# Putting both maps' score products side by side in a differential attention: a decoder trunk on one Trainium2 core

## The chip, the core and the metric

The kernel runs on one core of one Trainium2 chip. A core has a tensor engine (PE in the profile, with its weight loads as PEld), a vector engine (DVE), a scalar engine (ACT), a GpSimd engine (POOL), and a queue of transfers issued by SyncE (SP). Each engine works through its own instructions in order and waits on semaphores for the others. [...] The metric is the device time of the whole program in microseconds (us), the median of several executions.

## The reference

Two decoder layers over 512 tokens of width 1024, float32, batch 1. Layer 0 is a gated recurrence, layer 1 a differential attention; each is followed by a mixture of 32 experts of which every token uses two. What matters here is the attention (8 heads, each with two maps of 64 dimensions, rows in blocks of 128):

```python
def diff_attention(h, w_in, w_out, lam_params, subln_w, lambda_init):
    ...
    for blk in range(S // Q):
        q0, kend = blk * Q, (blk + 1) * Q
        s = jnp.einsum('bhmqd,bhmkd->bhmqk', q[:, :, :, q0:kend], k[:, :, :, :kend]).astype(jnp.float32) * scale
        mask = (q0 + jnp.arange(Q))[:, None] >= jnp.arange(kend)[None, :]
        p = jax.nn.softmax(jnp.where(mask, s, -jnp.inf), axis=-1)
        a = p[:, :, 0] - lam * p[:, :, 1]
        outs.append(jnp.einsum('bhqk,bhkv->bhqv', a, v[:, :, :kend]))
    ...
    return o.transpose(0, 2, 1, 3).reshape(B, S, D).astype(h.dtype) @ w_out
```

## The kernel before

The order of all instructions is written out by hand with Python generators: `weave(main, (other, rate))` advances `other` by `rate` steps for each step of `main`, and each step appends instructions to the engines' queues. Nothing is reordered later.

The attention (`attention`, lines 583 to 733) works on two halves of four heads. A projection block (`proj`, line 215, and `proj_rows`, line 241) makes Q, K or V of one half from weights that ACT (line 179) and POOL or DVE (line 180) split into a high and a low part. `heads(half, ...)` works through 16 units of a half. A unit is one head `h` and one block `t` of 128 query rows (t = 0 to 3), and so has n = 128(t+1) key columns. Each half has four units of each size, 32 units in all. At step u of `heads` the queues receive:

- `score(u)`: for each of the two maps m, the product of 64 dimensions (partitions 64m to 64m+63 of `qT` and `kT`, line 633), followed by the causal mask, a bf16 product of the identity with a triangle of -1e30 that is added to the last 128 columns (line 634). Each map has a PSUM tile, a bank, of its own. A float32 product shows as two weight loads and two MATMUL records.
- `mix(u-2)`: DVE combines both maps' probabilities (lines 653 to 655), PE transposes the result (line 659), ACT copies it out (line 661).
- `probs(u)`: DVE takes the maximum of each map (line 644), scales it (line 645), ACT makes the exponentials with their sums (line 647). The second exponential is the last to read a unit's score tiles.
- `av(u-3)`: PE multiplies by V (line 668), ACT copies and squares (lines 671, 673).

In half 0 the units go head by head, t = 0 to 3 each, and all use the two tiles `sc0` and `sc1`, so that a unit's first product waits until the unit before has read its first map, and the second product until it has read the second. They are woven with the Q and K projections of half 1 (line 724). In half 1 the units go by t, all four heads of a size together; the first 8 or so are woven with the V projection (line 730), the rest run without a projection beside them (line 731). From its ninth unit on, half 1 uses six tiles in turn (`sc0`, `sc1`, `pj0` to `pj3`). After the last unit come the rest of the output weights, the norm and `mix_out`, then the experts of layer 1.

In the experts (lines 1204, 1205, 1222, 1223), blocks of at most 64 tokens use 64 columns of the array at a time: the products of line 1222 write the first 64 partitions of one bank, those of line 1223 the last 64 of another, one after the other in the queue:

```python
for k in range(NF):
    b, e = (k == 0), (k == NF - 1)
    nc.tensor.matmul(y[0][0:n, :], gt[:, k, 0:n], w[NC1 + k][:, 0:512], start=b, stop=e)
    nc.tensor.matmul(y[1][P - n:P, :], gt[:, k, 0:n], w[NC1 + k][:, 512:1024], start=b, stop=e)
```

Of the kernel before, what the change touches and what calls it, by code (L numbers as in the profile page):

```python
# [9 lines left out]
F32 = mybir.dt.float32  # L10
# [11 lines left out]
S = 512  # L22
P = 128
# [89 lines left out]
def weave(main, *others):  # L113

    due = [0.0] * len(others)
    for n, _ in enumerate(main):
        for i, (g, rate, *start) in enumerate(others):
            due[i] += rate if n >= sum(start) else 0.0
            while due[i] >= 1.0:
                due[i] -= 1.0  # L120
                if next(g, "end") == "end":
                    due[i] = -1e9
# [25 lines left out]
def chain(*gens):  # L148
    for g in gens:
        yield from g  # L150
# [432 lines left out]
def attention(K, pool, psum, st, hh, hl, o):  # L583

    nc = K.nc
    nlam, wn, cos, sin, ident_b, causal = K.attn
    ss, rs = ([K.wp.tile([P, NT, 4], F32, name=f"{n}{i}") for i in range(2)] for n in ("ss", "rs"))
    v = [pool.tile([P, NT, 512], F32, name=f"v{i}") for i in range(2)]
    T, due = {}, []

    def qk_done(name, half):
        def f(t, ps):
            if t == 0:
                T[name, half] = pool.tile([P, 4, S], F32, name=name, bufs=2)
            dst = T[name, half]
            pv = ps.rearrange("p (m w d) -> p m w d", m=8, w=2)
            tt = K.stage.tile([P, 1024], F32, name="raw", bufs=12)
            ta, tb = (tt[:, 512 * j:512 * j + 512].rearrange("p (m w d) -> p m w d", m=8, w=2) for j in range(2))
            for x, f in ((ta, cos), (tb, sin)):
                nc.vector.tensor_tensor(x, pv, f[:, t, None, None, :].to_broadcast([P, 8, 2, 32]), OP.mult)  # L600
            for w in range(2):
                nc.gpsimd.tensor_tensor(ta[:, :, w, :], ta[:, :, w, :], tb[:, :, 1 - w, :],
                                        OP.add if w else OP.subtract)
            tf = tt[:, 0:512]

            def turn():
                tr = psum.tile([P, 4, P], F32, name="tr")
                for h in range(4):
                    nc.tensor.transpose(tr[:, h, :], tf[:, h * P:(h + 1) * P], K.ident)
                nc.scalar.activation(dst[:, :, t * P:(t + 1) * P], tr, AF.Copy)  # L610

            K.later.append(turn)
        return f

    def v_done(half):
        def f(t, ps):
            nc.scalar.activation(v[half][:, t, :], ps, AF.Copy)
        return f

    def heads(half, units, tags, after):  # L620

        qT, kT = T["qT", half], T["kT", half]
        U = {}

        def score(u):
            h, t = units[u]
            names = tags(u)
            n = (t + 1) * P
            sc = []
            for m in range(2):  # L630
                r = slice(64 * m, 64 * m + 64)
                x = psum.tile([P, S], F32, name=names[(2 * u + m) % len(names)])
                nc.tensor.matmul(x[:, 0:n], qT[r, h, t * P:n], kT[r, h, 0:n], start=True, stop=False)
                nc.tensor.matmul(x[:, t * P:n], ident_b, causal, start=False, stop=True)
                sc.append(x)
            U[u] = (h, t, n, sc)

        def probs(u):
            h, t, n, sc = U[u]
            z = pool.tile([P, 10], F32, name="st", bufs=4)  # L640
            mx, nm, l, c, cc = (z[:, 2 * j:2 * j + 2] for j in range(5))
            p = K.stage.tile([P, 1024], F32, name="raw", bufs=12).rearrange("p (m n) -> p m n", m=2)
            for m in range(2):
                nc.vector.tensor_reduce(mx[:, m:m + 1], sc[m][:, 0:n], AX.X, OP.max)
            nc.vector.tensor_scalar(nm, mx, -0.125, None, op0=OP.mult)
            for m in range(2):
                nc.scalar.activation(p[:, m, 0:n], sc[m][:, 0:n], AF.Exp, bias=nm[:, m:m + 1], scale=0.125,
                                     accum_out=l[:, m:m + 1])
            U[u] = (h, t, n, p, l, c, cc)

        def mix(u):
            h, t, n, p, l, c, cc = U[u]
            nc.vector.reciprocal(c, l)
            nc.vector.scalar_tensor_tensor(cc[:, 0:1], c[:, 1:2], nlam, l[:, 0:1], op0=OP.mult, op1=OP.mult)
            nc.vector.scalar_tensor_tensor(p[:, 0, 0:n], p[:, 1, 0:n], cc[:, 0:1], p[:, 0, 0:n],
                                           op0=OP.mult, op1=OP.add)
            tr = psum.tile([P, 4, P], F32, name="tr")
            for s in range(t + 1):
                nc.tensor.transpose(tr[:, s, :], p[:, 0, s * P:(s + 1) * P], K.ident)
            aT = pool.tile([P, 4, P], F32, name="aT", bufs=2)  # L660
            nc.scalar.activation(aT[:, 0:t + 1, :], tr[:, 0:t + 1, :], AF.Copy)
            U[u] = (h, t, c, aT)

        def av(u):
            h, t, c, aT = U.pop(u)
            po = psum.tile([P, S], F32, name="po")
            for s in range(t + 1):
                nc.tensor.matmul(po[:, 0:P], aT[:, s, :], v[half][:, s, h * P:(h + 1) * P],
                                 start=(s == 0), stop=(s == t))
            c0 = (4 * half + h) * P  # L670
            nc.scalar.activation(o[:, t, c0:c0 + P], po[:, 0:P], AF.Copy, scale=c[:, 0:1])
            sq = pool.tile([P, P], F32, name="sq")
            nc.scalar.activation(sq, po[:, 0:P], AF.Square, scale=c[:, 0:1], accum_out=ss[half][:, t, h:h + 1])
            if u in after:
                due.append(after[u])

        for u in range(len(units) + 3):
            if u < len(units):
                score(u)
            if 0 <= u - 2 < len(units):  # L680
                mix(u - 2)
            if u < len(units):
                probs(u)
            if 0 <= u - 3:
                av(u - 3)
            yield

    def finish(half, t0, n, table=False):
        sv, rv = (x[half][:, t0:t0 + n, :].rearrange("p t h -> p (t h)") for x in (ss, rs))
        nc.vector.tensor_scalar(sv, sv, 1.0 / P, EPS, op0=OP.mult, op1=OP.add)  # L690
        yield from rsqrt_steps(K, K.wp, rv, sv, 4 * n, table)
        yield
        for t in range(t0, t0 + n):
            for h in range(4):
                c = slice((4 * half + h) * P, (4 * half + h + 1) * P)
                nc.vector.scalar_tensor_tensor(o[:, t, c], o[:, t, c], rs[half][:, t, h:h + 1], wn,
                                               op0=OP.mult, op1=OP.mult)
            yield

    def finishing(n):  # L700
        for _ in range(n):
            while not due:
                yield
            yield from due.pop(0)

    def turning(steps):

        for _ in steps:
            for turn in K.later[0:2]:
                turn()  # L710
            del K.later[0:2]
            yield

    def block(done):
        return proj(K, st, psum, hh, hl, True, done)

    K.scratch = Ctx()
    K.scratch.lng, K.scratch.lnb = (v[1].rearrange("p t n -> p (t n)")[:, j * D:(j + 1) * D] for j in range(2))
    yield proj_rows(K, st, psum, hh, hl, qk_done("qT", 0))
    weave(chain(block(qk_done("kT", 0)), block(v_done(0))), (K.rows, 0.25))  # L720
    drain(K.rows)
    s0 = heads(0, [(h, t) for h in range(4) for t in range(NT)], lambda u: ["sc0", "sc1"], {15: finish(0, 0, 4)})
    K.lo_eng = nc.gpsimd
    weave(chain(block(qk_done("qT", 1)), block(qk_done("kT", 1))), (s0, 0.7))
    drain(s0)
    s1 = heads(1, [(h, t) for t in range(NT) for h in range(4)],
               lambda u: ["sc0", "sc1"] + ([f"pj{i}" for i in range(4)] if u >= 8 else []),
               {4 * t + 3: finish(1, t, 1) for t in range(NT - 1)})
    f, w = finishing(NT), wout(K, 1)
    weave(turning(proj_rows(K, st, psum, hh, hl, v_done(1))), (s1, 0.9), (f, 1.0))  # L730
    weave(s1, (w, 0.8), (f, 1.0))
    drain(f)
    K.wsteps = chain(iter([None]), w, finish(1, NT - 1, 1, True))
# [977 lines left out]
```

## Time and profile before

| | |
|---|---|
| time, median of 3 runs | 1717.24 us (1713.92 to 1721.87) |
| the profiled execution | 1717.6 us, its span 1715.8 us |
| PE busy | 1464.7 us, 85% of the span |
| DVE, ACT, POOL busy | 657.4, 362.9, 317.4 us (38%, 21%, 18%) |
| mean granted clock of the tensor engine | 0.92 of full speed |
| first score product to the last unit's product with V | 1071.8 to about 1255 us |

The times of stages are counted from the start of the span. [...] A timeline line has start and duration in us, the engine, the line of the code, the operation, what it writes and reads, its shape and how many equal records are merged in it; in brackets is how long the engine sat idle before it and what ended that. Ends of MATMUL records are modelled, so the text counts from start to start.

### The profile page before, as it was taken

The page shows a single profiled execution, that of the slowest core. Times are in us where ns is not written, and L with a number is a line of the kernel's source. Part 1 is how long each engine was busy: PE and PEld are TensorE (multiplying, and loading weights), DVE is VectorE, ACT ScalarE, POOL GpSimd, SP SyncE. Part 2 cuts the span into 40 slices and gives each one's busy share as a digit, 9 for nine tenths or more (in the row PEclk, how much of TensorE's full clock was granted, in tenths as well). Part 3 has the DMA queues.
Part 4 walks back from the last instruction along what each step waited for, and adds up shares of the span by engine and source line. Part 5 has one row for each costly group of instructions (what it writes and reads, how often), then busy time and mean ns, then how long its engine had stood idle before and what let it go on. Part 6 is the DMA issues. An engine that isn't in the chain of part 4 may idle for free. (4 is left out here: it accounts for less than half of the span.)

```text
span 1715.8 us, 22446 instructions
## 1 busy us (share of the span) xinstructions
PE 1464.7 (85%) x6488; PEld 869.9 (51%) x6488; DVE 657.4 (38%) x1486; ACT 362.9 (21%) x754; POOL 317.4 (18%) x299
## 2 busy tenths in 40 slices
PE   6999999988776989988888389999989569989870
PEld 3767776757643434333333268566467334444340
DVE  5335556648750111111112162545577521111105
ACT  2331232123210001101111143453532101000100
POOL 2000000005310011111111145222154110110102
PEclk9899999989878999999999699999589779999985
DMA  9565555443758398999998424012035785783913
GB/s 351 218 198 185 178 170 176 158 154 108 261 221 299 91 341 312 347 396 380 378 384 308 130 94 136 16 59 87 25 135 172 272 289 183 261 290 126 333 33 110
DMA packets 102765, 358.72 MB, mean 209 GB/s; under 512 B 14512, under 2 KB 15408, under 8 KB 102480
## 3 DMA queue, kind: packets, MB, share of 16 engines
q1 hardware_dynamic: 90320, 322.65, 51.7%
q0 software_dynamic: 11008, 31.57, 7.1%
q8 instruction: 121, 1.98, 0.5%
q14 instruction: 164, 1.34, 0.2%
q10 hardware_dynamic: 1152, 1.18, 0.2%
HBM read 368.15 MB, written 25.26 MB: 229 GB/s over the span
## 5 line engine op out<-in xcount | busy, mean ns | idle before, releaser
L1211 DVE SCALAR_TENSOR_TENSOR g<-s,w_it,a 64x512 f32<-64x512 f32 (+1 forms) x34 | 25.4, 748 | 390.9 <-PE a L1205 249.6
L1210 ACT ACTIVATE s<-a 64x512 f32<-64x512 f32 (+1 forms) x40 | 23.8, 594 | 484.0 <-PE a L1204 329.6
L1204 PE MATMUL a<-raw,xT 128*64 128x512 f32 (+1 forms) x224 | 111.1, 618 | 15.4 <-DMA mw_hl<-in_blob_dram 6.6
L1231 POOL DMA_INDIRECT xd<-yo,idx_t x32 | 47.0, 1469 | 402.8 <-DVE yo L1228 240.3
L1205 PE MATMUL a<-raw,xT 128*64 128x512 f32 (+1 forms) x224 | 110.0, 614 | 2.3 <-DVEq L1291 2.0
L1204 PE MATMUL a<-mw_w_lo,xT 128*64 128x512 f32 (+1 forms) x112 | 64.5, 695 | 42.2 <-PEq L1159 36.0
L1227 DVE TENSOR_TENSOR yo<-y,g 64x512 f32<-64x512 f32 (+1 forms) x40 | 27.4, 686 | 186.0 <-PE y L1222 117.2
L215 PE MATMUL pj<-w_hi,hh 128*128 128x512 f32 x224 | 94.6, 422 | 0.0
L215 PE MATMUL pj<-w_lo,hh 128*128 128x512 f32 x224 | 88.8, 396 | 2.1 <-DVE w_lo L180 2.1
L215 PE MATMUL pj<-w_hi,hl 128*128 128x512 f32 x224 | 88.2, 394 | 0.0
L180 DVE TENSOR_TENSOR w_lo<-raw,w_hi 128x1024 fp32r<-128x1024 f32 x44 | 55.2, 1271 | 51.5 <-ACT w_hi L179 51.5
L179 ACT ACTIVATE w_hi<-raw 128x1024 fp32r<-128x1024 f32 x64 | 66.3, 1054 | 30.1 <-DMA xd<-yo,cur 25.3
L180 POOL TENSOR_TENSOR w_lo<-raw,w_hi 128x1024 fp32r<-128x1024 f32 x20 | 48.7, 2446 | 112.8 <-ACT w_hi L179 103.0
L1205 PE MATMUL a<-mw_w_lo,xT 128*64 128x512 f32 (+1 forms) x112 | 62.8, 680 | 5.8 <-DVEq L1291 3.1
L1204 PEld LDWEIGHTS a<-raw,xT 128*64 128x64 f32 (+1 forms) x224 | 35.7, 167 | 63.1 <-issue 45.8
L1184 POOL DMA_INDIRECT xg<-h2d,idx_t x36 | 35.7, 991 | 171.2 <-issue 84.1
L316 POOL DMA_DIRECT2D mod<-ada_b x16 | 8.1, 507 | 312.8 <-DVE ada_b L315 312.8
L1216 ACT ACTIVATE gT<-pg 128x512 f32<-128x512 f32 x40 | 23.9, 598 | 184.4 <-PEq L1291 95.7
L1195 PE MATMUL tp<-ident,xg 128*128 128x128 f32 x336 | 47.8, 288 | 17.5 <-DMA xg<-h2d,idx 11.5
L1204 PE MATMUL a<-mw_hh,xT 128*64 128x512 f32 (+1 forms) x96 | 49.5, 646 | 15.1 <-PEq L1159 8.6
L1195 PEld LDWEIGHTS tp<-ident,xg 128*128 128x128 f32 x336 | 39.2, 147 | 42.7 <-issue 23.1
L463 PEld LDWEIGHTS sc<-q,k 128*128 128x128 f32 x448 | 56.5, 191 | 4.3 <-issue 0.6
(424 smaller groups left out, 3315.9 us busy)
## 6 DMA issues: line engine op xcount, KB each, us to landing
raw<-in_blob_dram SPq DMA_DIRECT2D x168, 512.0 KB
raw<-in_ada_w_dram SPq DMA_DIRECT2D x96, 512.0 KB
mw<-in_blob_dram SPq DMA_DIRECT2D x96, 512.0 KB
mw_hh<-in_blob_dram SPq DMA_DIRECT2D x56, 512.0 KB
mw_hl<-in_blob_dram SPq DMA_DIRECT2D x56, 512.0 KB
mw_w_hi<-in_blob_dram SPq DMA_DIRECT2D x48, 512.0 KB
mw_w_lo<-in_blob_dram SPq DMA_DIRECT2D x48, 512.0 KB
raw<-in_hgrn_w_in_dram SPq DMA_DIRECT2D x32, 512.0 KB
```

Of the source, the lines that this page charges most:

```text
L179: nc.scalar.activation(hi, raw2, AF.Copy)
L180: K.lo_eng.tensor_tensor(lo, raw2, hi.bitcast(F32), OP.subtract)
L215: nc.tensor.matmul(ps[i], h[:, k, c], w[:, kk, :], start=b, stop=e)
L463: nc.tensor.matmul(sc[:, b, 0:64], k[:, b * P:(b + 1) * P], qv[:, b, :, 1, :], start=True, stop=True)
L1184: nc.gpsimd.indirect_dma_start(out=x[0:n, :], out_offset=None, in_=h2d, in_offset=bass.IndirectOffsetOnAxis(ap=idx[0:n, :], axis=0), bound ...
L1195: nc.tensor.transpose(tp[half][:, j, :], x[:, k * P:(k + 1) * P], K.ident)
L1204: nc.tensor.matmul(a1[0:n, :], xt[:, k, 0:n], w[k][:, 0:FF], start=b, stop=e)
L1205: nc.tensor.matmul(a3[P - n:P, :], xt[:, k, 0:n], w[k][:, FF:2 * FF], start=b, stop=e)
L1211: nc.vector.scalar_tensor_tensor(g[0:n, :], s[0:n, :], wt[0:n, :], a3[P - n:P, :], op0=OP.mult, op1=OP.mult)
L1216: nc.scalar.activation(gt, pg, AF.Copy)
L1227: nc.vector.tensor_tensor(o[0:n, 0:512], y[0][0:n, :], g2[0:n, 0:512], OP.mult)
L1231: nc.gpsimd.indirect_dma_start(out=xd, out_offset=bass.IndirectOffsetOnAxis(ap=idx[0:n, :], axis=0), in_=o[0:n, :], in_offset=None, bounds ...
```

## The change

Both PSUM tiles are taken first; then the two score products are queued one behind the other, then the two mask products. Operands, tiles and the number of instructions stay as they were, and so does everything outside `score`. Before, PE's queue for a unit read: product 0, mask 0, product 1, mask 1. After: product 0, product 1, mask 0, mask 1.

```diff
             n = (t + 1) * P
-            sc = []
-            for m in range(2):
+            sc = [psum.tile([P, S], F32, name=names[(2 * u + m) % len(names)]) for m in range(2)]
+            for m, x in enumerate(sc):
                 r = slice(64 * m, 64 * m + 64)
-                x = psum.tile([P, S], F32, name=names[(2 * u + m) % len(names)])
                 nc.tensor.matmul(x[:, 0:n], qT[r, h, t * P:n], kT[r, h, 0:n], start=True, stop=False)
+            for x in sc:
                 nc.tensor.matmul(x[:, t * P:n], ident_b, causal, start=False, stop=True)
-                sc.append(x)
             U[u] = (h, t, n, sc)
```

## Rows read from the trace of the kernel before

**Rows 1.** Busy time by engine, granted clock and DMA in five stretches.

```profile
core 0: us, PE busy (x) PEld busy (x) DVE busy (x) ACT busy (x) POOL busy (x), PEclk, DMA share, GB/s
1071.80:1145.10 73.30, 68.50 (x317) 43.26 (x317) 38.93 (x96) 36.29 (x117) 19.25 (x14) 1.00 0.12 36
...
1169.50:1202.10 32.60, 32.60 (x154) 22.86 (x152) 17.42 (x71) 12.63 (x50) 2.10 (x1) 1.00 0.33 100
1202.10:1206.00 3.90, 2.56 (x12) 1.32 (x12) 2.19 (x9) 2.32 (x10) 0.00 (x0) 0.98 0.80 252
1206.00:1249.00 43.00, 42.65 (x109) 21.51 (x108) 23.69 (x81) 22.45 (x68) 9.38 (x4) 0.50 0.01 2
1249.00:1262.00 13.00, 6.10 (x41) 5.20 (x40) 12.41 (x27) 9.55 (x21) 7.27 (x3) 0.89 0.36 116
```

**Rows 2.** Timeline of PE, a unit of t = 1 in half 0.

```profile
1075.46 0.70 PE L633 MATMUL sc<-kT,qT 64*128 64x256 f32 x2 [0.98 <-ACT raw L647]
1076.09 0.23 PE L634 MATMUL sc<-causal,ident_b 128*128 128x128 bf16 x1
1076.24 0.70 PE L633 MATMUL sc<-kT,qT 64*128 64x256 f32 x2
1076.87 0.23 PE L634 MATMUL sc<-causal,ident_b 128*128 128x128 bf16 x1
1076.91 0.47 PE L215 MATMUL pj<-w_hi,hh 128*128 128x512 f32 x1
```

**Rows 3.** Timeline of PE, product and mask at t = 0.

```profile
1169.57 0.49 PE L633 MATMUL sc<-kT,qT 64*128 64x128 f32 x2
1169.98 0.23 PE L634 MATMUL sc<-causal,ident_b 128*128 128x128 bf16 x1
```

**Rows 4.** Timeline of PE, product and mask at t = 3, full clock.

```profile
1142.70 1.12 PE L633 MATMUL sc<-kT,qT 64*128 64x512 f32 x2
1143.75 0.23 PE L634 MATMUL sc<-causal,ident_b 128*128 128x128 bf16 x1
```

**Rows 5.** Timeline of PE at half clock, t = 2 and then t = 3.

```profile
1206.43 1.65 PE L633 MATMUL sc<-kT,qT 64*128 64x384 f32 x2
1208.01 0.29 PE L634 MATMUL sc<-causal,ident_b 128*128 128x128 bf16 x1
...
1234.64 2.07 PE L633 MATMUL pj<-kT,qT 64*128 64x512 f32 x2
1236.64 0.29 PE L634 MATMUL pj<-causal,ident_b 128*128 128x128 bf16 x1
1236.87 2.07 PE L633 MATMUL pj<-kT,qT 64*128 64x512 f32 x2
```

**Rows 6.** Timeline of DVE and ACT, the unit whose first product starts at 1079.83.

```profile
1080.94 0.56 DVE L644 TENSOR_REDUCE st<-sc 128x1 f32<-128x384 f32 x1 [2.40 <-PE sc L634]
1081.94 0.56 DVE L644 TENSOR_REDUCE st<-sc 128x1 f32<-128x384 f32 x1 [0.44 <-PE sc L634]
...
1082.79 0.58 ACT L647 ACTIVATE raw<-sc,st 128x384 f32<-128x384 f32 x1 [0.45 <-DVE st L653]
1083.36 0.57 ACT L647 ACTIVATE raw<-sc,st 128x384 f32<-128x384 f32 x1
```

**Rows 7.** Waits of PE's weight loads, 1071.8 to 1262: total us, times, longest.

```profile
PEld sc L633 <- ACT raw L647: 4.7, 9, 1.4
```

**Rows 8.** Timeline of PE, second product of half 1's ninth unit.

```profile
1204.53 0.91 PE L633 MATMUL pj<-kT,qT 64*128 64x384 f32 x2 [1.34 <-ACT v L617]
```

**Rows 9.** Timeline of PE, experts of layer 1, products on 64 columns each.

```profile
1422.61 0.64 PE L1222 MATMUL y<-mw_w_hi,gT 128*64 128x512 f32 x1
1422.61 0.64 PE L1223 MATMUL y<-mw_w_hi,gT 128*64 128x512 f32 x1
1423.09 0.59 PE L1222 MATMUL y<-mw_w_hi,gT 128*64 128x512 f32 x1
1423.09 0.59 PE L1223 MATMUL y<-mw_w_hi,gT 128*64 128x512 f32 x1
```

## The prediction

> **What bounds the kernel now.** I read the table of stretches first, to see which engine sets the pace where the change works [rows 1]. I call 1071.8 to 1145.1 stage A (half 0's sixteen units among projections), 1169.5 to 1202.1 stage C (half 1's first eight units among projections), and 1206 to 1249 stage D (half 1's last seven units, no projections). PE is busy 68.50 of 73.30 us in A, all of 32.60 in C and 42.65 of 43.00 in D. DVE, the next, has 23.69 us in D. In C and D a microsecond taken from PE is a microsecond of the program, until DVE's sum is reached; in A it is one where PE does not wait. DMA moves 2 GB/s in D, so no transfer sets its end. The granted clock is 1.00 in A and C and 0.50 in all of D: the same product takes twice as long there.
>
> Then the timeline of PE, start to start, for one unit of each kind. A product and its own mask are never close together: with t = 1, product 0 starts at 1075.46, its mask at 1076.09, product 1 at 1076.24, its mask at 1076.87, and the next work 0.04 us later [rows 2]. So D(1) = 0.63 us from product to mask, and 0.15 us from a mask to the product behind it. D(0) = 0.41 [rows 3], D(3) = 1.05 [rows 4], so D grows 0.21 us for 128 columns, over two passes, and D(2) is 0.84. At half clock D(2) = 1.58, D(3) = 2.00, and mask to product 0.23 [rows 5]. Of D about 0.20 does not grow with the columns (0.63 less two times 0.21). I read it as the exposed weight load and the emptying of the array before a mask on 128 rows; the 0.15 behind a mask, where a projection comes in after 0.04, is the same price the other way.
>
> Last the waits around a unit: who frees the score tiles [rows 6, 7] and the one long wait before D [rows 8].
>
> **The change part by part.** Nothing is added or removed: 128 score records, 64 masks, the same loads, no DMA. Three things move.
>
> First, product 1 stands directly behind product 0. They use different halves of the array's 128 rows (operand shape 64*128 in every score row) and different banks. Whether they run at the same time is not in this trace, since a mask on all rows always stood between. The nearest row is the other way of halving the array: lines 1222 and 1223 use 64 columns each, follow each other in the queue, and their records start together, at 1422.61 and again at 1423.09, 0.48 us apart, and that from the first pass on [rows 9]. If halves of rows do as halves of columns do, product 1 costs nothing, and a unit's pair takes D instead of D + 0.15 + D. Bounds for product 1's cost: nothing [rows 9], or its full streaming time, D less 0.20. I take nothing.
>
> [...]
>
> Second, the masks stand together. The second one's distance from the first is not in the trace; it lies between 0.04 (mask to a projection) and 0.15 (mask to a half-row product) [rows 2]. Both masks are on 128 rows, which is nearer to the first, so 0.08; 0.12 at half clock. A unit then saves D + 0.15 - 0.08: 0.48, 0.70, 0.91 and 1.12 us for t = 0 to 3; at half clock 1.58 + 0.23 - 0.12 = 1.69 and 2.11.
>
> Third, mask 0 now waits for whatever product 1 waits for. Behind it in PE's queue are both masks, the transposes and the products with V, and DVE's first maximum waits for mask 0. In A this matters: product 1's tile is freed by the second exponential of the unit before, 0.57 us after the first [rows 6], a wait that product 0 used to cover.
>
> Stage A: four units of each size give 4 × (0.48 + 0.70 + 0.91 + 1.12) = 12.8 us if PE never waits. But take the unit of 1079.83. Its second maximum started at 1081.94; now it can start when the first ends, 1080.94 + 0.56 = 1081.50, so the exponentials, and with them the tiles, come 0.44 earlier, while PE would be ready 0.91 earlier. And the next unit's product 1 stands 0.57 behind product 0. Such a handover gives back 0.47 + 0.57 = 1.0 us. Score loads waited for an exponential nine times before [rows 7], about half of them hardly; I take five handovers, 5.0 us, with 0 and 9 as bounds. A saves 7.8 us (3.8 to 12.8).
>
> Stage C: PE had no idle time, so no exponential was late: 4 × (0.48 + 0.70) = 4.7 us. The ninth unit (1202.1 to 1206) saves nothing: its product 1 waited 1.34 us for ACT to empty a projection's tile [rows 8], and still does, now with mask 0 behind it; that delays the unit's first maximum, on DVE, which has 2.19 us to do in 3.90 [rows 1].
>
> Stage D: three units of t = 2 and four of t = 3 at half clock: 3 × 1.69 + 4 × 2.11 = 13.5 us. PE then has 29.5 us of work, above DVE's 23.7 and ACT's 22.5, so it still sets the pace. If the clock came back to 1.00, PE's work would be some 15 us, DVE would set it, and D could lose at most 43.0 - 23.7 = 19.3 us. The clock fell right behind the one stretch with a wait in it and stayed at 0.50 with PE busy throughout; it was back while products with V and transposes ran, with PE busy 6.10 of 13 us [rows 1]. Shorter scores leave those a larger share. I take 15.0, nearer to the value at half clock, which is what the rows show.
>
> What follows D (the last norms, output weights, experts) is ordered behind the last unit, and DMA is idle before it, so it moves forward whole. Sum: 7.8 + 4.7 + 15.0 = 27.5 us. The profiled execution took 1717.6, of which 1715.8 is the span, and is 0.4 above the median; 1717.6 - 27.5 - 0.4 gives 1690 us.
>
> **The rivals.** *Half an overlap.* Records start in queue order: passes 0a, 0b, 1a, 1b, so that only 0b and 1a coincide. Product 1 adds one pass, 0.105(t+1) us, twice that at half clock. C saves 4.7 - 1.3 = 3.4, D 13.5 - 5.2 = 8.3, A about 12.8 - 4.2 - 4.0 = 4.6: in all 16.3, 1701 us. Against it: [rows 9].
>
> *No overlap: the change doesn't do what it could.* Product 1 then adds 0.21(t+1), and a unit saves only the emptying between them: D + 0.15 - 0.08 - (D - 0.20) = 0.27 us, 0.43 at half clock. C 2.2, D 3.0, A 4.3 less five handovers: the first maximum now starts 0.64 later at t = 2, the second 0.2 later instead of 0.27 earlier, 0.5 each, which leaves 1.9. In all 7.1, 1710 us, which counts as no change. For it: no row with two half-row products side by side.
>
> *Slower by the clock.* [...] A's handovers make PE wait more often, and before D a wait came just ahead of the fall. At half clock C's remaining 28 us of PE work take about 25 more (D(2) goes from 0.84 to 1.58); alone that gives 1715, no change. If the fall comes at 1145, the 24.4 us of projections up to 1169.5 cost 22 more: 47 - 27.5, so 1737. It decides from 36 us lost to it on (27.5 and 8.6). Against it: the clock is 1.00 through A, with 4.8 us of PE idle in it, and through C [rows 1].
>
> **How the numbers follow.** Full overlap 0.70 (1690; its own range, with A, the second mask and D at their bounds, 1680 to 1698), half overlap 0.08, none 0.14, slower by the clock 0.05; 0.03 for a gain that a later wait takes back. The three runs lie 0.46% apart, so 0.5% (8.6 us) is about what can be told from no change. Faster: 0.70 + 0.08 + 0.02 of "none" = 0.80; same 0.14; slower 0.06. 1680 to 1709 holds full overlap but for a tail, half overlap, and a third of none: 0.8.
>
> **What would show it.** In the timeline of PE both score products of a unit start within some 0.02 us, and the first mask D behind them; a first mask at D + 0.21(t+1) means none, one pass behind D means half. The two masks lie 0.04 to 0.15 apart. The maxima of a unit follow each other without a gap. In the stretches, C falls from 32.6 to about 28 us and D from 43 to between 24 and 30, with its PEclk telling which. Waits of score loads on exponentials grow in A, and A shrinks by less than the other two for its 12.8. The prediction is wrong if row halves don't overlap, if the clock falls before D, or if A's handovers eat all of its share.

## The result and the profile after

| | before | after |
|---|---|---|
| median of 4 runs each | 1719.55 us (1713.92 to 1722.48) | 1697.22 us (1696.62 to 1698.02) |
| ratio, 95% interval | | 0.9874 [0.9846, 0.9903] |
| span of the profiled execution | 1715.76 us | 1695.43 us |

The kernel became 22 us faster. The forecast was 1690 us, its range 1680 to 1709. The total lies in the range, but it is made of other parts than the forecast's, and the rest of this document is about them. One of the six executions of the kernel that the table below calls "low halves on DVE, a step late" took 2948.69 us and is left out of its median.

In the code after, the score products stand on line 632 (633 before) and the masks still on 634; the lines behind them are one lower than before: maximum 643, scaling 644, exponentials 646, mix 654, transposes 658, products with V 667, the output stage's transposes 808. The first view is the table of stretches of after, which answers to [rows 1]: half 0's first and second eight units, stage C, the ninth unit of half 1, and stage D in two pieces (up to the first product of the last unit, and from there to the first transpose of the output stage). PEclk is the granted clock as a share of full speed; half clock is 0.50.

```profile
core 0: us, PE busy (x) PEld busy (x) DVE busy (x) ACT busy (x) POOL busy (x), PEclk, DMA share, GB/s
1070.00:1101.10 31.10, 28.41 (x151) 19.36 (x150) 15.88 (x43) 16.34 (x52) 6.13 (x3) 1.00 0.06 17
1101.10:1138.70 37.60, 30.81 (x160) 22.25 (x160) 21.12 (x53) 18.78 (x62) 12.67 (x11) 0.91 0.14 43
1165.70:1193.20 27.50, 27.50 (x153) 20.20 (x152) 16.71 (x69) 12.58 (x50) 2.00 (x1) 1.00 0.37 118
1193.20:1199.00 5.80, 3.96 (x13) 2.08 (x12) 2.71 (x12) 2.57 (x10) 0.00 (x0) 0.75 0.54 182
1199.00:1225.90 26.90, 18.32 (x88) 11.05 (x87) 23.40 (x64) 17.45 (x52) 7.03 (x3) 0.82 0.00 1
1225.90:1242.80 16.90, 9.23 (x52) 7.31 (x52) 15.40 (x36) 11.17 (x30) 8.14 (x4) 0.77 0.00 0
```

C is still all PE (27.50 of 27.50). D is not: PE is busy 27.55 of 43.8 us, DVE 38.80. For comparison the same two pieces of D in before:

```profile
1206.40:1241.20 34.80, 34.80 (x87) 17.27 (x86) 19.01 (x66) 17.49 (x53) 7.04 (x3) 0.50 0.00 1
1241.20:1255.80 14.60, 12.26 (x52) 8.18 (x51) 10.98 (x21) 10.74 (x30) 7.90 (x4) 0.69 0.00 0
```

PE's work in D fell from 47.06 to 27.55 us, by more than forecast, since the clock came back as well (0.82 and 0.77, against 0.50 and 0.69). The time fell by 5.6 us only: the first piece fell by 7.9 us, the second grew by 2.3. DVE's work with the same instructions rose from 29.98 to 38.80 us: that is where much of the gain went.

The next view is the timeline of PE in after, a unit of t = 2 and one of t = 3 at full clock:

```profile
1077.26 0.92 PE L632 MATMUL sc<-kT,qT 64*128 64x384 f32 x4
1078.11 0.28 PE L634 MATMUL sc<-causal,ident_b 128*128 128x128 bf16 x2
1078.23 0.28 PE L658 MATMUL tr<-ident,raw 128*128 128x128 f32 x1
...
1208.46 1.13 PE L632 MATMUL sc<-kT,qT 64*128 64x512 f32 x4
1209.52 0.29 PE L634 MATMUL sc<-causal,ident_b 128*128 128x128 bf16 x2
```

The four records of a pair (x4) take 1.13 us at t = 3, as long as the two records of one product before (1.12 [rows 4]). The masks begin 0.85 and 1.06 us behind the start of the pair, which is D(2) and D(3) of one product before (0.84, 1.05). The two products run at the same time. In the single records behind the first row the four passes start at 0.00, 0.01, 0.43 and 0.43 us. The two passes of one product of this size start 0.43 us apart in before, so I read the second record as product 1's first pass: it starts before product 0's second.

The stages of each run, in us, from its own profile, are told in one table. A stage goes from first product to first product: half 0 up to half 1's first product, C, the ninth unit, D up to the first transpose of the output stage; "behind" is from there to the span's end.

| profile | half 0 | C | ninth unit | D (up to the last unit + from it on) | behind | span |
|---|---|---|---|---|---|---|
| before | 97.75 | 32.55 | 4.32 | 34.79 + 14.53 = 49.32 | 460.0 | 1715.76 |
| before, once more | 97.78 | 32.52 | 4.14 | 34.79 + 14.69 = 49.48 | 460.2 | 1714.61 |
| after | 95.65 | 27.58 | 5.82 | 26.85 + 16.84 = 43.69 | 452.7 | 1695.43 |
| after, once more | 94.72 | 27.54 | 4.59 | 26.34 + 16.64 = 42.98 | 457.2 | 1698.70 |
| new order in half 0 only | 95.54 | 32.55 | 4.07 | 31.31 + 16.01 = 47.32 | 456.4 | 1705.66 |
| new order in half 1 only | 99.91 | 27.58 | 5.93 | 26.87 + 16.86 = 43.73 | 456.2 | 1706.08 |
| low halves on DVE | 95.59 | 27.54 | 5.90 | 32.24 + 28.19 = 60.43 | 453.4 | 1713.38 |
| GpSimd's subtraction in four | 94.66 | 27.58 | 4.48 | 25.96 + 16.52 = 42.48 | 453.5 | 1691.67 |
| the same in before | 100.01 | 32.55 | 4.08 | 34.78 + 14.04 = 48.82 | 454.2 | 1711.83 |
| low halves on DVE, a step late | 94.69 | 27.58 | 4.47 | 22.38 + 17.98 = 40.36 | 452.0 | 1689.59 |
| other order of tiles | 95.61 | 27.58 | 2.90 | 26.33 + 16.65 = 42.98 | 456.5 | 1697.87 |
| fewer units per projection step | 104.60 | 27.54 | 4.47 | 26.44 + 16.62 = 43.06 | 456.8 | 1709.10 |
| late low halves and other order of tiles | 94.68 | 27.58 | 2.90 | 21.90 + 16.06 = 37.96 | 452.8 | 1686.57 |
| both products on the same rows | 97.82 | 30.20 | 5.92 | 29.57 + 17.80 = 47.36 | 476.6 | 1728.12 |

Against the profile of before, after gained 2.1 us in half 0, 5.0 in C and 5.6 in D, and lost 1.5 in the ninth unit: 11.2 us in the attention. The other 9.1 of 20.3 us are 1.8 ahead of it and 7.3 behind it, where no instruction differs. The repeated profiles give 14.1 in the attention and 3.0 behind it, and lose 1.2 ahead of it.

### The profile page after: what moved, and what is told of

It reads as the page before. It is cut to its first block, busy times and chain, and to the rows that moved or that the text cites. A ratio compares the mean times of both kernels' runs of the same rounds, so it can differ in the third digit from the quotient of the medians.

```text
span 1695.4 us, 22446 instructions
## 1 busy us (share of the span) xinstructions
PE 1426.7 (84%) x6488; PEld 856.4 (51%) x6488; DVE 658.9 (39%) x1486; ACT 362.8 (21%) x754; POOL 314.9 (19%) x299
## 5 line engine op out<-in xcount | busy, mean ns | idle before, releaser
L1209 ACT ACTIVATE s<-a 64x512 f32<-64x512 f32 (+1 forms) x40 | 23.7, 593 | 480.2 <-PE a L1203 324.4
```

## The experiments

### Each half by itself

The first two keep the new order in one half and give the other the old one.

```diff
+            if half == 0:
+                sc = [psum.tile([P, S], F32, name=names[(2 * u + m) % len(names)]) for m in range(2)]
...
+            else:
+                sc = []
+                for m in range(2):
...
+                    nc.tensor.matmul(x[:, 0:n], qT[r, h, t * P:n], kT[r, h, 0:n], start=True, stop=False)
+                    nc.tensor.matmul(x[:, t * P:n], ident_b, causal, start=False, stop=True)
```

Half 0 only:

> The new order in half 0 alone (the 16 units among the Q and K projections); half 1 keeps product, mask, product, mask. [...] If the loss in half 0 was an accident of one execution, the stage takes about 90 us (97.75 less the 7.8 of the prediction) and the whole about 8 us less.

Half 1 only (`if half == 1:`):

> The new order in half 1 alone. If the gain is made there, the stage from half 1's first score product to the first transpose of the output stage takes about 77 us against 86.2 before, half 0's stage 97 to 98, and the whole is 11 to 18 us below before, most of the 22 us of the full change. If the two halves share the gain evenly, it is about 10 us below.

Measured: half 0 only 1708.58 us, 0.9956 [0.9937, 0.9975] of before; half 1 only 1707.08 us, 0.9933 [0.9907, 0.9958]. Before's median beside them was 1718.58, so by the medians they gain 10.0 and 11.5 us, by the ratios 7.6 and 11.5. The sum, 21.5 or 19.1, is about what both together gain: I see no sign that one half pays for the other. The stages of half 1 are the same whether half 0 has the new order or not (C 27.58 both times, D 43.73 against 43.69), so D's shortfall is D's own. Half 0 gains 2.2 us in its own stage, which takes 95.54 us and not about 90: that speaks against an accident of one execution. The whole gained more than that stage. Most of the rest of the first run lies in stages where its code is that of before (2.1 ahead of the attention, 2.0 in D, 3.6 behind). In its D the granted clock was back at 1.00 from 1229.7 us on, 28 us into the stage, in before only from 1250.3, 44 us into it: D of the old order is not one number (47.32 to 49.48 in four profiles). Nor is its half 0: in the second run it took 99.91 us, where 97 to 98 were expected, which I come back to.

### Both products on the same rows

What part of the gain is the overlap, and what is only the grouping? Here map 1 reads the partitions of map 0. Map 1's scores are then those of map 0, and the two products no longer use different halves of the rows; order, sizes and masks stay.

```diff
-                r = slice(64 * m, 64 * m + 64)
+                r = slice(0, 64)
```

> The new order, but both products read the first 64 partitions, so that map 1's scores are those of map 0 and the two products cannot use different halves of the array; instructions, sizes and order stay. If the gain is overlap, only the emptying between the kinds of products is saved: half 1's first eight units take about 30.4 us (32.55 before less 8 times 0.27), against 27.6 with the change, and the first mask stands 0.21 us per 128 columns later than with the change. If the gain is the fewer switches between half-row and full-row products, they take about 27.6 us again. Only the attention's stages count in this run, since other probabilities send other tokens to the experts.

The timeline of PE in this run, a unit of t = 2:

```profile
1077.80 1.55 PE L632 MATMUL sc<-kT,qT 64*128 64x384 f32 x4
1079.29 0.28 PE L634 MATMUL sc<-causal,ident_b 128*128 128x128 bf16 x2
```

The mask follows after 1.49 us instead of 0.85: product 1 adds 0.64 us, which is 0.21 × 3, its full streaming time, the price that the rival "no overlap" gave it. C took 30.20 us, 2.35 less than before (that rival: 2.2). Since C of after is 27.58, its gain of 5.0 us is 2.35 from the grouping alone, 0.29 us a unit, where 0.27 was priced (I read it as fewer switches between half and whole rows; what a switch consists of is not shown), and 2.6 from overlap. With other scores the tokens go to other experts, so this run's total (1729.99 us) says nothing.

### The disputed cost in D: GpSimd beside DVE

Where do DVE's 8.8 us come from? The view of one line gives the shortest, median and longest duration in ns, first for the scaling of the maxima in D of before, then in 1201 to 1232 of after:

```profile
L645 DVE TENSOR_SCALAR st<-st x8: 169/170/578, 1206.2 to 1246.5; 128x2 f32<-128x2 f32 x8
```

```profile
L644 DVE TENSOR_SCALAR st<-st x7: 169/1836/2301, 1202.1 to 1229.1; 128x2 f32<-128x2 f32 x7
```

An instruction on 2 columns, 0.17 us long, takes up to 2.30 us. The timeline of after shows beside what:

```profile
1207.46 1.02 DVE L643 TENSOR_REDUCE st<-pj 128x1 f32<-128x384 f32 x2 [0.26 <-ACT sq L672]
1208.45 2.34 POOL L180 TENSOR_TENSOR hl<-raw,hh 128x1024 fp32r<-128x1024 f32 x1 [40.75 <-ACT hh L179]
1208.51 2.30 DVE L644 TENSOR_SCALAR st<-st 128x2 f32<-128x2 f32 x1
1210.91 0.58 ACT L646 ACTIVATE raw<-pj,st 128x384 f32<-128x384 f32 x1 [2.16 <-DVE st L644]
1212.98 0.48 PE L658 MATMUL tr<-ident,raw 128*128 128x128 f32 x2 [3.18 <-DVE raw L654]
```

GpSimd subtracts a low half of the output weights (line 180) from 1208.45 to 1210.79. DVE's scaling begins 0.06 us later and ends with it, at 1210.81. The exponential waits 2.16 us for it, and PE 3.18 us for the mix. Four such scalings in the stretch took 2.30, 2.04, 2.03 and 1.84 us, each beside one of GpSimd's four subtractions there: 7.5 us more than seven times 0.17. Behind the last unit a mix (2.87 us at 1234.15) and a scaling of the norm (2.32 us at 1236.95) stood in the same way, but there before has two such operations as well (below).

Before had the same subtractions in D, the first from 1218.89 to 1221.24. The timeline of DVE there:

```profile
1220.10 0.56 DVE L644 TENSOR_REDUCE st<-pj 128x1 f32<-128x384 f32 x1 [1.17 <-PE pj L634]
1220.69 0.58 DVE L645 TENSOR_SCALAR st<-st 128x2 f32<-128x2 f32 x1
```

The subtraction ran while DVE waited for the second mask. The maximum beside it kept its 0.56 us, and the scaling met only the subtraction's last half microsecond; it, too, ended with it. The three subtractions behind it, up to 1245.96, met only maxima, which kept their 0.69 us. Behind the last unit it was otherwise in before too: its last three subtractions stood beside three steps of the norm.

```profile
1250.59 2.33 DVE L690 TENSOR_SCALAR ss<-ss 128x4 f32<-128x4 f32 x1
1252.95 2.28 DVE L89 TENSOR_SCALAR rs<-ss 128x4 int32<-128x4 int32 x1
1255.27 2.27 DVE L90 TENSOR_SCALAR rs<-rs 128x4 int32<-128x4 int32 x1
```

So what is new in after are above all the four scalings. There both maxima follow each other at once, and the scaling comes right when ACT has released the subtraction: the change itself moved the two together.

In these rows, then, the scalings stood until the subtraction's end (2.30 us instead of 0.17), and the maxima beside one kept their 0.56 and 0.69 us. What holds a scaling is not in the trace; I take it to be the subtraction.

If this is the cause, the cost must go when the subtraction no longer stands beside the scalings. The first try moves the low halves to DVE where they stand:

```diff
     weave(turning(proj_rows(K, st, psum, hh, hl, v_done(1))), (s1, 0.9), (f, 1.0))
+    K.lo_eng = nc.vector
     weave(s1, (w, 0.8), (f, 1.0))
```

> The change, and the low halves of the output weights that are split during half 1's last units made on the vector engine (1.2 us each) instead of GpSimd (2.35 us each). If half 1's missing gain is the vector engine's small operations standing still while GpSimd subtracts (four of 2 us each, and more behind the last unit), the stage from half 1's first product to the output stage falls from 77.1 to about 70 us and the whole by 4 to 8 us. If the vector engine's own sum of work is what bounds these units, eight more operations of 1.2 us on it make the stage 4 to 9 us longer.

Measured 1715.16 us, 0.9984 [0.9968, 1.0] of before. D took 60.43 us, more than in any other kernel. It meets neither expectation, since it brings a wait of its own (timeline of DVE):

```profile
1208.88 1.23 DVE L180 TENSOR_TENSOR hl<-raw,hh 128x1024 fp32r<-128x1024 f32 x1 [2.91 <-ACT hh L179]
```

The subtraction itself takes 1.23 us on DVE, but each one stood 2.9 to 4.7 us at the head of DVE's queue until ACT had written the high half. ACT does that behind the exponentials, so the next unit's DVE work waited with it. The fault is the place in the queue, not the engine.

The second try cuts GpSimd's subtraction in four, so that DVE can come in between:

```diff
-            K.lo_eng.tensor_tensor(lo, raw2, hi.bitcast(F32), OP.subtract)
+            for i in range(self.parts):
+                c = (slice(None),) if self.parts == 1 else (slice(None), i // 2, slice(256 * (i % 2), 256 * (i % 2) + 256))
+                K.lo_eng.tensor_tensor(lo[c], raw2[c], hi.bitcast(F32)[c], OP.subtract)
...
+        w.parts = 4 if l else 1
```

> The change, and each GpSimd subtraction of the output weights' low halves cut into four of a quarter of the size (about 0.6 us each), in the same place. If the vector engine's small operations stand still behind a whole GpSimd subtraction, each of them now waits at most some 0.6 us instead of 2: the units 26 to 32 of the attention (26.9 us from the first product of one to that of the last) take 22 to 24 us, half 1's stage falls from 77.1 to 71 to 74 us, and the whole by 3 to 6 us. If the vector engine's own work bounds them, nothing changes by more than 1 us.

The same edit in the kernel before is the control, since there PE sets the pace of D:

> The kernel before, with the GpSimd subtractions cut in four as in the run on the changed kernel. Before, the tensor engine was the bound of half 1's last units and the vector engine had slack, so that cutting them should be worth little there: half 1's stage 83 to 86 us against 86.2, the whole within 3 us of before. If it gains as much here as on the changed kernel, the standing still was no part of what the change lost.

Measured: in after 1694.60 us, 0.987 [0.9846, 0.9894]; D's first piece went from 26.85 (26.34 in the second profile) to 25.96, where 22 to 24 were expected. In before 1713.85 us, 0.9979 [0.996, 0.9999], and that piece stayed at 34.78 (34.79). The totals settle nothing: by the ratios the cut took 3.6 us off before and under 1 us off after (2.6 by the medians). By D's first piece it took nothing off before and 0.4 to 0.9 us off after. That is the direction that the collision asks for, but hardly more than after's two profiles differ by. The cut gained so little because DVE meets the next quarter again (timeline of the cut kernel, whose scaling is on line 648):

```profile
1205.82 0.68 DVE L648 TENSOR_SCALAR st<-st 128x2 f32<-128x2 f32 x1
1206.41 2.62 DVE L699 SCALAR_TENSOR_TENSOR o<-o,rs,wn 128x128 f32<-128x128 f32 x4
...
1205.75 2.87 POOL L183 TENSOR_TENSOR hl<-raw,hh 128x256 fp32r<-128x256 f32 x4 [40.06 <-ACT hh L180]
```

The scaling now costs 0.68 instead of 2.30 us, but the four small operations behind it, 1.13 us in after, take 2.62, and the four quarters together take 2.87 instead of 2.34 us. So the standing still moves on to other operations, and isn't cured in this way. What it costs is left to the third try.

The third try takes GpSimd out of the stretch without the wait of the first: DVE does each low half one step after its high half was issued to ACT.

```diff
+            if self.late is None:
+                K.lo_eng.tensor_tensor(lo, raw2, hi.bitcast(F32), OP.subtract)
+            else:
+                self.late.append((lo, raw2, hi))
...
+    def low():
+        while late:
+            lo, raw2, hi = late.pop(0)
+            K.nc.vector.tensor_tensor(lo, raw2, hi.bitcast(F32), OP.subtract)
...
             w.ahead(n)
+            low()
             yield
```

> The change, with the low halves of the output weights made on the vector engine, each one step after its high half, so that GpSimd is idle in half 1's last units and the vector engine never waits at the head of its queue for the scalar engine's high half. If GpSimd's hold on the vector engine is what half 1's last units lose (four holds of about 2 us against four operations of 1.14 us), the units 26 to 32 take 21 to 24 us instead of 26.85, half 1's stage 70 to 74 us instead of 77.1 and the whole 3 to 7 us less than the change. If the vector engine's own sum or the scalar engine's chain bounds them, the stage stays at 76 us or more.

Measured 1693.67 us (five executions, 1690.75 to 1697.69), 0.9863 [0.9835, 0.9892]. The two groups of DVE in 1201 to 1232 of this kernel (scaling on line 658, low halves on 205; busy us, mean ns, idle before):

```profile
L205 DVE TENSOR_TENSOR hl<-raw,hh 128x1024 fp32r<-128x1024 f32 x4 | 4.9, 1224 | 0.0
...
L658 DVE TENSOR_SCALAR st<-st 128x2 f32<-128x2 f32 x7 | 1.2, 169 | 0.2
```

All seven scalings are back at 0.169 us, and these four low halves wait for nothing. D's first piece falls from 26.85 to 22.38 us, the whole of D by 3.3 (its second piece grows by 1.1), though DVE now does the subtractions too: 1.22 us each there cost less than about 2.0 us of standing still. The clock does not explain it: it was 0.77 in that piece, against 0.82 in after.

### The ninth unit

Its product 1 waits for a projection's tile, as the forecast took from [rows 8], and mask 0 behind it. The timeline of after:

```profile
1195.98 1.54 PE L632 MATMUL pj<-kT,qT 64*128 64x384 f32 x2 [1.84 <-ACT v L617]
```

The forecast gave it nothing; it lost 1.5 us in one profile of after and 0.3 in the other. Here the tiles from the ninth unit on are taken in another order, so that it gets two projection tiles that ACT empties earlier:

```diff
-               lambda u: ["sc0", "sc1"] + ([f"pj{i}" for i in range(4)] if u >= 8 else []),
+               lambda u: ["pj2", "pj3", "sc0", "sc1", "pj0", "pj1"] if u >= 8 else ["sc0", "sc1"],
```

> The change, and the six score tiles of half 1 taken in another turn, so that the ninth unit gets the two projection tiles that are emptied first and no longer waits for the last one. If that wait sets the unit's 5.8 us and brings on the fall of the clock at 1196 us, the unit takes about 3 us and half 1's stage falls from 77.1 to 72 to 74 us. If the tensor engine only waits for something else then (the second maximum, the transposes), the stage falls by less than 1 us.

The wait is gone (timeline of PE, this kernel):

```profile
1195.46 0.92 PE L632 MATMUL pj<-kT,qT 64*128 64x384 f32 x4
```

The unit takes 2.90 us instead of 5.82. D is 42.98, as in the second profile of after, and the total, 1699.82 us, 0.9895 [0.9871, 0.9919], can't be told from the change's.

### Handovers in half 0

Fewer units per projection step should leave each exponential more time before the next unit wants its tile.

```diff
-    weave(chain(block(qk_done("qT", 1)), block(qk_done("kT", 1))), (s0, 0.7))
+    weave(chain(block(qk_done("qT", 1)), block(qk_done("kT", 1))), (s0, 0.56))
```

> The change, with half 0's units spread over all projection steps (0.56 units a step instead of 0.7), so that more projection products stand between two units. If half 0's missing gain is the wait of a unit's products for the exponentials of the unit before, it goes: the stage takes 90 to 92 us instead of 95.65 and the whole 3 to 5 us less. If it is the vector engine's queue (rotations of Q and K ahead of the mixing of probabilities) or the clock alone, the stage keeps 94 us or more.

Measured 1705.45 us, 0.9936 [0.9913, 0.996]. The waits of PE in half 0 by releaser (total us, times, longest), first in after, then in this run:

```profile
PE tr L658 <- DVE raw L654: 4.8, 3, 2.2
PE sc L632 <- ACT raw L646: 4.7, 7, 1.1
```

```profile
PE tr L658 <- DVE raw L654: 12.9, 5, 4.5
...
PE sc L632 <- ACT raw L646: 1.1, 4, 0.5
```

The handovers nearly went (4.7 to 1.1 us), and the stage grew to 104.6 us, with more waits for the mix in their place. As a repair this failed. It also says that handovers alone don't set half 0's time.

### Both kernels again, and the best version

Each kernel was profiled a second time, to see what of the stages repeats:

> The kernel before, profiled a second time, for how much of a stage differs between executions of the same program. If what came before and after the attention (9.1 of the 20.3 us between the two profiles) belongs to the executions, the stage from the output stage on takes 454 to 458 us here instead of 460.0, and the attention's two stages together 183 to 187 us. If it belongs to the change, the stage from the output stage on is again about 460 us.

> The changed kernel, profiled a second time. [...]

They took 1716.48 and 1700.48 us. C and D's first piece repeat within 0.5 us, half 0 within 0.9. "Behind" of before is 460.2 again, which by its expectation speaks for the change; that of after moves by 4.5 us (452.7 and 457.2), which speaks for the execution. The falls of the clock in half 0 of after did not come at the same units: two stretches at half clock in the first profile (from 1104.0 and from 1117.6), one in the second (from 1126.6).

Last, the late low halves and the other order of tiles together, with both diffs as above:

> The change with both repairs of half 1 together: low halves of the output weights on the vector engine, each a step behind its high half, and the score tiles in the other turn. If the two waits are separate, the ninth unit takes 2.9 us and the units 26 to 32 about 22.4, half 1's stage 70 to 71 us against 72.4 and 73.5 with one repair each, and the whole 1688 to 1693 us. If the vector engine bounds both, the ninth unit's gain comes back as a longer wait behind it and the stage stays at 72 us or more.

Measured 1688.96 us (1688.44 to 1691.23), 0.9842 [0.9815, 0.9868] of before's 1715.42. Its five times lie below all of after's (1696.62 to 1698.02), though the two intervals of the ratios overlap. Half 1's stage is 68.4 us, less than the 70 to 71 expected. D's two pieces, in stretches:

```profile
1195.80:1217.70 21.90, 13.85 (x89) 8.23 (x88) 19.23 (x62) 17.19 (x52) 0.00 (x0) 1.00 0.06 24
1217.70:1233.70 16.00, 8.31 (x51) 6.59 (x50) 14.53 (x47) 11.73 (x31) 0.00 (x0) 0.89 0.00 1
```

The granted clock is 1.00 through D's first piece, and D takes 37.96 us, with DVE busy 33.75 of them.

## Why the prediction held, and where it did not

The direction and the range were right, and so was the mechanism, the case that was held likeliest. By its own steps:

**Product 1 costs nothing: right.** It starts 0.42 us ahead of product 0's second pass at t = 2, and the pair takes as long as one product. The rival "half an overlap", with the passes in queue order, would have put it behind; the four starts (0.00, 0.01, 0.43 and 0.43 us) decide against it. The mask follows after D, and with both products on the same rows after D + 0.21(t+1), as the rival priced it.

**Masks: right.** In the single records a unit's second mask starts 0.07 us behind the first at full clock and 0.08 at half clock; forecast 0.08 and 0.12.

**Stage C: right.** 4.7 forecast, 5.0 measured, clock 1.00, PE without a pause.

**Stage A: 7.8 forecast, 2.1 measured** (3.1 in the second profile). The handovers were sized about right. They show in two places. PE's waits for exponentials in half 0 rose from 1.4 to 4.7 us. And where product 1 has to wait behind product 0, the pair is longer: a unit of t = 3 like this one takes 1.68 instead of 1.13 us.

```profile
1080.83 1.68 PE L632 MATMUL sc<-kT,qT 64*128 64x512 f32 x4 [0.93 <-ACT raw L646]
```

Seven pairs are longer than an undelayed one, by 0.34, 0.55, 0.09, 0.31, 0.55 and, at t = 0, twice 0.48 us. With the 3.3 that makes 6.1 us; 5.0 was forecast. What had no term is the rest: PE waits 1.6 us more for DVE's mix (4.8 against 3.2) and 0.6 for Q, and two stretches of 3.4 us at half clock (0.51 and 0.52), where this profile of before had 1.00 throughout. If these cost about half their length, 3.4 us (an estimate), then 12.8 - 6.1 - 2.2 - 3.4 is 1.1, and the other 1.0 is unexplained by this sum, though C, too, gained 0.3 more than its pairs were priced at.

The other profiles in the table sharpen this. With half 0 as in after there are eight: four have two such stretches and take 95.54 to 95.65 us, four have one and take 94.66 to 94.72. So two of them cost 0.9 us more than one, less than the estimate's 1.7. The old order has such stretches too: its two profiles of before have none (97.75 and 97.78), but the two other kernels with the old order in half 0 ("new order in half 1 only" and "the same in before") have one each, from about 1110, and take 99.91 and 100.01. With one stretch on either side the new order gains 5.3 us in half 0; the 2.1 and 3.1 above compare profiles that have such stretches with ones that have none. One of after's two stretches begins at 1117.6, where the last of the waits for DVE's mix ended:

```profile
1111.74 0.63 PE L658 MATMUL tr<-ident,raw 128*128 128x128 f32 x4 [2.21 <-DVE raw L654]
1117.58 0.42 PE L658 MATMUL tr<-ident,raw 128*128 128x128 f32 x1 [2.08 <-DVE raw L654]
```

That is a small share of what the rival "slower by the clock" told. That waits bring these stretches about is read from their places alone, which did not repeat in the second profile; it is not shown.

**Stage D: 15.0 forecast, 5.6 measured (6.5 in the second profile). This term is the mis-sized one.** The step that failed is "above DVE's 23.7 and ACT's 22.5, so it still sets the pace". PE's work fell by 19.5 us, since the clock came back, and DVE did become the bound, as the step's other end foresaw: in D of after PE waits 14.6 us for DVE's mixes, in D of before not at all. But the price of that end was wrong: DVE's sum was read off a stretch in which PE set the pace, and there GpSimd's subtractions ran while DVE waited. Once DVE waits little, the same instructions take 38.80 instead of 29.98 us. With GpSimd out of the way D took 40.36, and 37.96 with the order of tiles as well, against a forecast of 34.3 (49.3 - 15.0). So of the 9.4 us missing, 3.3 (2.6 against the second profile of after) are the collision, net of the work that DVE takes over. Another 2.4 come with the order of tiles, most of them (1.9) in the second piece, where the clock is 0.89 instead of 0.73. The order of tiles alone did little for D (0.7 against one profile of after, nothing against the other), so the 2.4 hang on both. Over the last 3.7 DVE is busy 89% of D, with six low halves of 1.22 us in it; no run takes these apart.

**The ninth unit: 0 forecast, 0.3 to 1.5 lost,** by the wait that the forecast named: with mask 0 behind it the maximum comes later, and in the first profile of after the granted clock was 0.51 from that wait's end (1196) to 1201.

**What follows D "moves forward whole": not settled.** By stages the forecast is 16.3 us short (5.7 in A, 1.5 in the ninth unit, 9.4 in D, less 0.3 in C), but the span only 7.2 us (27.5 against 20.3), because 9.1 us came from stages with unchanged code. One piece of it is a wait just there, PE's for the last norm on DVE: 4.9 us before, 2.2 after (4.8 and 3.4 in the second profiles). It goes with the collision: three steps of that norm stood beside GpSimd in before, in after two (2.32 us at 1236.95 and 2.26 at 1241.89).

```profile
PE otp L808 <- DVE ol L811: 2.2, 1, 2.2
```

The rest is not the change's in any way I could show: the old order with a cut subtraction had 454.2 us behind D, where before has 460.0 and 460.2, and after has 452.7 and 457.2. The granted clock behind D goes with it: 0.90 at 454.2 and 452.7 us, 0.89 at 460.0 and 457.2. So it is luck that the forecast total is nearer to the measurement than its steps deserve.

## What to carry to other kernels

Products on different halves of the rows belong next to each other in the queue, with what needs all rows grouped behind them: in C, where PE sets the pace, that saved 2.6 us by overlap and 2.35 by grouping over eight units. Before a gain is booked, take the next engine's bound not from its busy time in a stretch where it waited, but from that time plus what other engines' work will do to it once it no longer waits (in D 29.98 us became 38.80 with the same instructions). And when work is moved to an in-order engine, give it a place behind its operand's arrival: the same subtraction on the same engine cost D 17 us in one place and gave it 3 a step later.

## What the runs showed of the hardware

A DVE instruction of 0.17 us took up to 2.30 us beside a GpSimd subtraction of 2.34 us, and ended with it; with no work on GpSimd all seven such instructions took 0.169 us. A maximum inside such a subtraction kept its 0.56 us (0.69 at 512 columns). Cutting the subtraction in four lengthened it from 2.34 to 2.87 us and spread the standing over more instructions. And two float32 products on half the rows each, of two passes each, interleave their passes: four records in the time of two (1.13 us at 512 columns, 1.12 for one product), and on the same rows the second product adds 0.64 us at 384 columns.
